# Alternating a group by seven products with a plain group in the feed-forward layers, and moving two splits ahead of top-k

## The chip, the cores and the metric

The kernel runs on one NeuronCore of a Trainium2 chip. The metric is the device time of one execution in microseconds, the median of several runs. A profiled execution gives the trace that is read here.

## The reference, cut to what matters

One input of 256 tokens by 1024 features goes through three layers in float32. Each layer is a mixer with a residual and then the same feed-forward form:

```python
def swiglu(h, w1, w3, w2):
    return (jax.nn.silu(h @ w1) * (h @ w3)) @ w2     # 1024 -> 2816 -> 1024
```

The first mixer is a sparse attention: four index heads score every pair of tokens, `top_k` keeps 64 keys of each query, and eight heads with two key/value groups attend to those keys. Beside it runs a pooling branch. The second mixer is a stick-breaking attention, the third joins a retention and a block-sparse attention. Only the first mixer and the three feed-forward layers are touched.

## The kernel before, in words

**Products in three passes.** Every float32 operand is held as a rounded high part and a low remainder, and `mm3` (L297) issues three matmuls: high by high, high by low, low by high, with the activations (128 by 128) as the loaded operand and 512 weight columns moving. Tokens come in two halves `h` of 128.

**The stream of weights.** `Stream` (L117 on) is a list of loads, sums and pieces written out ahead of time by the `plan_` functions. A load (L185) brings 1 MiB into one of four `w_raw` buffers through SyncE's queue. A piece is 128 by 1024 words: `_split` (L232) makes `w_hi` on ScalarE (L238) and `w_lo` on VectorE (L239), into five buffers each. `advance` (L244) issues loads, sums and splits up to four pieces ahead of the piece that TensorE takes; `tick` (L400) calls it and steps the background tasks (evacuations, transposes) that have come due. A framework then orders each engine's instructions by their place in the program, or by a raised priority, as its own timing finds them ready; each engine runs its list in that order.

**The feed-forward layer.** `ffn` (L602) walks `FF_GROUPS` (L517): hidden columns 0, 512 and 1536 are plain groups, 1024 and 2048 are groups by seven products, 2560 is a plain group of 256 columns. A plain group runs `proj` (L419) for `w1` and for `w3`: four pieces each, and each piece is used for both token halves, twelve matmuls. `gate` (L624) takes the silu on ScalarE, `up` (L629) multiplies on VectorE. Both projections take two of the four `acc` banks of PSUM.

A group by seven products (`block`, L563) treats the two token halves by the two halves of the 1024 inputs as a 2 by 2 matrix product with seven products in place of eight. Each has two pieces, and each piece is used once, six matmuls. Some products use sums of weight blocks. `add_block` (L168) plans three plain loads, the sums `s1` and `s3` and the growths `s2` and `s4`. A sum (L215) is a 1 MiB load by SyncE (L227) and a second one issued by GpSimd that accumulates onto it (L229). A growth is a VectorE addition in place (L222). Two sum buffers exist; `s1`, `s2` and `s4` are one buffer in turn, `s3` is the other. The order of products is 1, 5, 6, 2, 3, 7, 4; `s2` feeds product 6, `s4` feeds product 4. Sums of token blocks (`token_sums`, L530, fourteen VectorE and four ScalarE operations) are made once a layer, after group 0. `snap` and `result` (L651, L656) combine the banks. `turn` (L610) transposes a finished group through the two `misc` banks, in two steps two ticks apart.

**The sparse layer** (L925). It projects the index part, then keys and values (`kv`, L997), queries (`q`, L1015) and the pooling input. `top` (L983) is a chain of eight rounds of max and match-and-replace per token half on VectorE (L989, L990), then the mask (L996). `heads_T` (L689) transposes keys or queries through a `misc` bank and splits them (`kT`, `qT`; ScalarE and VectorE L318).

Of the kernel before, what the change touches and what calls it, by code (L numbers as in the profile page):

```python
# [23 lines left out]
F32 = mybir.dt.float32  # L24
# [5 lines left out]
P = 128  # L30
# [85 lines left out]
class Stream:  # L116
# [51 lines left out]
    def add_block(self, wl, cl, wr, cr):  # L168

        h = KD // 2  # L170
        b11, b12, b21, b22 = (wl, 0, h, cl, 512), (wr, 0, h, cr, 512), (wl, h, h, cl, 512), (wr, h, h, cr, 512)
        l11, l22, l21 = (self._load_of(*b) for b in (b11, b22, b21))
        s1 = self._sum_of(b12, b11)
        s3 = self._sum_of(b12, b22)
        s2 = self._grow(s1, l22)
        s4 = self._grow(s2, l21)
        for q, src in ((1, l11), (5, s1), (6, s2), (2, l21), (3, l22), (7, s3), (4, s4)):
            for k in range(0, h, 2):
                self._piece(src, k * 512, 2, 512, (wl, q, k, cl))
# [89 lines left out]
class Kernel:  # L269
# [149 lines left out]
    def proj(self, n, w, c0, cols, evac, fresh=False, feed=None):  # L419
# [4 lines left out]
        accs = [self.ps_acc(), self.ps_acc()]  # L424
# [9 lines left out]
        while k < KD:  # L434
# [13 lines left out]
            k += kc  # L448
        for i, piece in enumerate(held):
            mms(1, *piece)  # L450
            if i < len(held) - 1:
                self.tick()
        self.run(evac(1, accs[1]))
        self.tick()

# [61 lines left out]
    FF_GROUPS = ((0, 512, False), (512, 512, False), (1024, 512, True), (1536, 512, False), (2048, 512, True), (2560, 256, False))  # L517

    def plan_ffn(self, w1, w3, w2):
        for c0, m, block in self.FF_GROUPS:  # L520
            if block:
                self.st.add_block(w1, c0, w3, c0)
            elif m == 512:
                self.plan_proj(w1, c0, m)
                self.plan_proj(w3, c0, m)
            else:
                self.plan_proj(w1, c0, 2 * m, beside=(w3, c0, m))
# [35 lines left out]
    def block(self, n, sums, wl, c0, wr, snap, result):  # L563
# [21 lines left out]
        after(snap, "x1", x)  # L585
        z = self.ps_acc()
        product(z, 5, True)
        after(snap, "z", z)
        product(x, 6, False)
        after(snap, "x2", x)  # L590
# [3 lines left out]
        product(z, 3, False)  # L594
        after(result, 1, 0, z)
        product(x, 7, False)
        after(snap, "x3", x)
        v = self.ps_acc()
        product(v, 4, True)
        after(result, 0, 1, v)  # L600

    def ffn(self, n, w1, w3, w2, evac):  # L602
        nc = self.nc
        with self.tc.tile_pool(name="ffn", bufs=1) as fp, self.tc.tile_pool(name="ffn2", bufs=2) as f2, \
# [16 lines left out]
            def plain(c0, m):  # L621
                sg, hid = [], []
# [16 lines left out]
                if m == 512:  # L639
                    self.proj(n, w1, c0, m, gate, fresh=c0 == 0)  # L640
                    self.proj(n, w3, c0, m, up)
                else:
                    self.proj(n, w1, c0, 2 * m, both)
                return hid

            def by_block(c0):
                sg = [f2.tile([P, 512], F32, name=f"sg{h}") for h in range(2)]
                hid = [f2.tile([P, 512], F32, name=f"hid{h}") for h in range(2)]
                home = {"x1": sg[0], "x2": hid[0], "x3": sg[1], "z": hid[1]}

                def snap(what, acc):  # L651
                    nc.scalar.copy(home[what], acc)
                    if what == "x3":
                        nc.vector.tensor_sub(hid[1], hid[1], sg[1])

                def result(side, h, acc):  # L656
                    if side == 0:
                        nc.vector.tensor_add(sg[h], acc, sg[h])
                        nc.scalar.activation(sg[h], sg[h], AF.Silu, scale=n["rstd"][:, h:h + 1])
                    else:  # L660
                        nc.vector.tensor_sub(hid[h], acc, hid[h])
                    if side == 1 or h == 1:
                        nc.vector.scalar_tensor_tensor(hid[h], hid[h], n["rstd"][:, h:h + 1], sg[h], op0=OP.mult, op1=OP.mult)

                self.block(n, sums, w1, c0, w3, snap, result)
                return hid

            made = False
# [755 lines left out]
```

## Time and profile before

| what | value |
|---|---|
| median of 3 runs | 1014.12 us (1014.04 to 1014.58) |
| the profiled execution, its own time | 1014.49 us |
| its span, first to last instruction | 1012.7 us |
| mean granted TensorE clock | 0.998 |
| busy: TensorE, VectorE, ScalarE, GpSimd | 995.3, 732.6, 597.5, 86.9 us |
| DMA moved | 193.35 MB, mean 191 GB/s |

A matmul's length in the trace overlaps the next one's; the step from start to start (0.227 to 0.233 us for 128 by 512) is what one costs.

### The profile page before, as it was taken

What the parts mean: (1) busy time and instruction counts of PE and PEld (TensorE: products, weight loads), DVE (VectorE), ACT (ScalarE), POOL (GpSimd) and SP (SyncE); (2) the same over time, 40 slices, a digit from 0 to 9 for tenths busy, and PEclk for the clock granted to TensorE, in tenths of its full rate; (3) what the DMA queues carried; (4) which work ended last, traced back from release to release, by engine and by line L of the source; (5) the groups of instructions that cost most, each with busy time, mean ns of one, the idle gap of its engine ahead of it and who ended that gap; (6) DMA issues with size and microseconds to landing.
All of it is one profiled execution on the core that took longest, in us unless ns stands there. A gap on an engine that the chain in (4) does not pass through costs nothing.

```text
span 1012.7 us, 12657 instructions
## 1 busy us (share of the span) xinstructions
PE 995.3 (98%) x4727; PEld 812.8 (80%) x4727; DVE 732.6 (72%) x1009; ACT 597.5 (59%) x896; POOL 86.9 (9%) x180
## 2 busy tenths in 40 slices
PE   8899999999999999999999999999999999999998
PEld 7677887788788888787878888888887888787886
DVE  6987789884467887789794467666777668879643
ACT  7566666653467876757574366675444465667431
POOL 2500101000030000200000024000020011010000
PEclk9999999999999999999999999999999999999999
DMA  8633959764564324955955536445434559395631
GB/s 298 234 123 104 301 182 281 235 230 168 166 208 167 125 86 136 290 196 178 279 192 193 197 131 208 151 166 202 173 124 173 186 207 307 133 294 198 246 127 42
DMA packets 90286, 193.35 MB, mean 191 GB/s; under 512 B 3440, under 2 KB 16368, under 8 KB 90224
## 3 DMA queue, kind: packets, MB, share of 16 engines
q1 hardware_dynamic: 83456, 179.36, 50.7%
q0 software_dynamic: 6336, 12.58, 6.9%
q8 instruction: 37, 0.61, 0.2%
q10 hardware_dynamic: 432, 0.59, 0.2%
q14 instruction: 25, 0.20, 0.1%
HBM read 191.48 MB, written 1.05 MB: 190 GB/s over the span
## 4 chain that ended last, share of the span: by engine, by line
PE 82%; ACT 8%; DVE 6%; issue 3%; POOL 1%; ACTq 0%; DVEq 0%
PE acc L475 27%; PE acc L303 15%; PE acc L302 15%; PE acc L301 15%; ACT w_hi L238 5%; PE misc L327 3%; DVE w_lo L239 1%; DVE w_sum L222 1%; ACT hT_hi L314 1%; PE misc L301 1%; PE misc L302 1%; PE z L301 1%; PE z L303 1%; PE misc L303 1%; PE z L302 1%
## 5 line engine op out<-in xcount | busy, mean ns | idle before, releaser
L239 DVE TENSOR_TENSOR w_lo<-w_raw,w_hi 128x1024 fp32r<-128x1024 f32 (+1 forms) x313 | 375.8, 1214 | 163.9 <-ACT w_hi L238 162.8
L238 ACT CAST w_hi<-w_raw 128x1024 fp32r<-128x1024 f32 (+1 forms) x313 | 323.5, 1045 | 244.8 <-PE acc L475 109.2
L301 PE MATMUL acc<-w_hi,xT_hi 128*128 128x512 f32 (+2 forms) x776 | 302.3, 392 | 1.1 <-ACT w_hi L238 1.1
L302 PE MATMUL acc<-w_lo,xT_hi 128*128 128x512 f32 (+2 forms) x776 | 301.5, 389 | 0.7 <-DVE w_lo L239 0.5
L303 PE MATMUL acc<-w_hi,xT_lo 128*128 128x512 f32 (+2 forms) x776 | 300.9, 388 | 0.0
L301 PEld LDWEIGHTS acc<-w_hi,xT_hi 128*128 128x128 f32 x776 | 146.2, 188 | 29.7 <-ACT w_hi L238 1.6
L303 PEld LDWEIGHTS acc<-w_hi,xT_lo 128*128 128x128 f32 x776 | 146.1, 188 | 29.3
L302 PEld LDWEIGHTS acc<-w_lo,xT_hi 128*128 128x128 f32 x776 | 146.2, 188 | 28.3 <-DVE w_lo L239 1.3
L475 PE MATMUL acc<-w_hi,hT_hi 128*128 128x512 f32 x264 | 105.1, 398 | 0.0
L475 PE MATMUL acc<-w_lo,hT_hi 128*128 128x512 f32 x264 | 104.1, 394 | 0.0
L475 PE MATMUL acc<-w_hi,hT_lo 128*128 128x512 f32 x264 | 86.9, 395 | 0.0
L238 ACT CAST w_hi<-w_sum 128x1024 fp32r<-128x1024 f32 x48 | 50.0, 1057 | 50.8 <-DVE w_sum L222 25.4
L239 DVE TENSOR_TENSOR w_lo<-w_sum,w_hi 128x1024 fp32r<-128x1024 f32 x48 | 58.1, 1221 | 21.6 <-ACT w_hi L238 21.1
L475 PEld LDWEIGHTS acc<-w_hi,hT_hi 128*128 128x128 f32 x264 | 49.6, 188 | 12.5
L475 PEld LDWEIGHTS acc<-w_hi,hT_lo 128*128 128x128 f32 x264 | 49.6, 188 | 11.7
L475 PEld LDWEIGHTS acc<-w_lo,hT_hi 128*128 128x128 f32 x264 | 49.6, 188 | 10.9
L318 DVE SCALAR_TENSOR_TENSOR xT_lo<-misc,gains,xT_hi 128x128 fp32r<-128x128 f32 (+1 forms) x84 | 27.9, 353 | 24.8 <-ACT xT_hi L317 24.7
L301 PE MATMUL acc<-w_hi,xs 128*128 128x512 f32 x96 | 40.1, 418 | 5.0 <-ACT w_hi L238 5.0
L303 PE MATMUL acc<-w_hi,xs 128*128 128x512 f32 x96 | 37.9, 395 | 0.0
L302 PE MATMUL acc<-w_lo,xs 128*128 128x512 f32 x96 | 37.8, 394 | 0.0
L317 ACT ACTIVATE xT_hi<-misc,gains 128x128 fp32r<-128x128 f32 (+1 forms) x84 | 29.0, 370 | 13.8 <-DVE xT_lo L318 9.0
L371 POOL TENSOR_TENSOR norm_s<-norm_ss 128x1 f32<-128x1 f32 x10 | 4.8, 479 | 343.9 <-ACT junk L367 343.8
(297 smaller groups left out, 1250.1 us busy)
## 6 DMA issues: line engine op xcount, KB each, us to landing
w_raw<-in_ffn_w_dram SPq DMA_DIRECT2D x58, 1024.0 KB, 5.1
w_raw<-in_w_in_dram SPq DMA_DIRECT2D x26, 1024.0 KB, 4.9
w_raw<-in_w_ffn_down_dram SPq DMA_DIRECT2D x11, 1024.0 KB, 5.0
w_raw<-in_w_ffn_gate_dram SPq DMA_DIRECT2D x10, 1024.0 KB, 5.5
w_sum<-in_ffn_w_dram SPq DMA_DIRECT2D x8, 1024.0 KB, 6.4
w_sum<-in_ffn_w_dram POOLq DMA_DIRECT2D x8, 1024.0 KB, 14.6
w_raw<-in_od_w_qkv_dram SPq DMA_DIRECT2D x8, 1024.0 KB, 5.1
w_raw<-in_w_ffn_up_dram SPq DMA_DIRECT2D x8, 1024.0 KB, 5.7
```

Of the source, the lines that this page charges most:

```text
L222: nc.vector.tensor_add(t, t, s["y"]["tile"])
L238: self.pin(nc.scalar.copy(hi, raw))
L239: self.pin(nc.vector.tensor_sub(lo, raw, hi.bitcast(F32)))
L301: self.pin(nc.tensor.matmul(out, ah, bh, start=start, stop=False, skip_group_check=True))
L302: self.pin(nc.tensor.matmul(out, ah, bl, start=False, stop=False, skip_group_check=True))
L303: self.pin(nc.tensor.matmul(out, al, bh, start=False, stop=stop, skip_group_check=True))
L314: nc.scalar.copy(hi, src)
L317: self.pin(nc.scalar.mul(hi, src, scale))
L318: self.pin(nc.vector.scalar_tensor_tensor(lo, src, scale, hi.bitcast(F32), op0=OP.mult, op1=OP.subtract))
L327: self.pin(self.nc.tensor.transpose(out, in_, self.ident))
L371: self.nc.gpsimd.tensor_tensor(s, n["ss"][:, h, 0:1], n["ss"][:, h, 1:2], op=OP.add)
L475: mm = lambda a, b, start, stop: self.nc.tensor.matmul(o, a, b, start=start, stop=stop, skip_group_check=True)
```

## The change

The work and the number of matmuls stay. The four 512-column groups after group 0 become two pairs: plain 512 with seven products 1024, and plain 1536 with seven products 2048. A pair's plan (`add_pair`) alternates one plain piece with one product (two pieces): plain, 1, plain, 5, plain, 3, plain, 2, plain, 6, plain, 7, plain, 4, plain. `proj` and `block` become generators that `ffn` steps in turn. The plain group of a pair accumulates in the two `z` banks (`ps_z`), the seven products in the four `acc` banks. The order of products is 1, 5, 3, 2, 6, 7, 4. The token sums start between the two projections of group 0. In the sparse layer `heads_T` raises the priority of the splits of keys and of queries.

```diff
--- before.py
+++ after.py
@@ -12,7 +12,7 @@


 import heapq
-from contextlib import ExitStack
+from contextlib import ExitStack, nullcontext

 import numpy as np

@@ -165,18 +165,26 @@
         for k in range(0, kc, step):
             self._piece(src, k * n, min(step, kc - k), n, (w, k0 + k, c0))

-    def add_block(self, wl, cl, wr, cr):
+    def add_pair(self, w1, w3, cp, cb):
+

         h = KD // 2
-        b11, b12, b21, b22 = (wl, 0, h, cl, 512), (wr, 0, h, cr, 512), (wl, h, h, cl, 512), (wr, h, h, cr, 512)
-        l11, l22, l21 = (self._load_of(*b) for b in (b11, b22, b21))
+        load = lambda w, k0, c: self._load_of(w, k0, h, c, 512)
+        a0, l11, l22, a1 = load(w1, 0, cp), load(w1, 0, cb), load(w3, h, cb), load(w1, h, cp)
+        l21, b0, b1 = load(w1, h, cb), load(w3, 0, cp), load(w3, h, cp)
+        b11, b12, b22 = (w1, 0, h, cb, 512), (w3, 0, h, cb, 512), (w3, h, h, cb, 512)
         s1 = self._sum_of(b12, b11)
         s3 = self._sum_of(b12, b22)
         s2 = self._grow(s1, l22)
         s4 = self._grow(s2, l21)
-        for q, src in ((1, l11), (5, s1), (6, s2), (2, l21), (3, l22), (7, s3), (4, s4)):
-            for k in range(0, h, 2):
-                self._piece(src, k * 512, 2, 512, (wl, q, k, cl))
+        factors = ((1, l11), (5, s1), (3, l22), (2, l21), (6, s2), (7, s3), (4, s4))
+        plain = [(src, w, k0 + k, k) for src, w, k0 in ((a0, w1, 0), (a1, w1, h), (b0, w3, 0), (b1, w3, h)) for k in (0, 2)]
+        for i, (src, w, k0, k) in enumerate(plain):
+            self._piece(src, k * 512, 2, 512, (w, k0, cp))
+            if i < len(factors):
+                q, src = factors[i]
+                for k in range(0, h, 2):
+                    self._piece(src, k * 512, 2, 512, (w1, q, k, cb))

     @staticmethod
     def _part(w, k0, kc, c0, n):
@@ -416,12 +424,16 @@
         for k0 in range(0, KD, kc):
             self.st.add(w, k0, min(kc, KD - k0), c0, n, beside)

-    def proj(self, n, w, c0, cols, evac, fresh=False, feed=None):
-
-
-
-
-        accs = [self.ps_acc(), self.ps_acc()]
+    def proj(self, *args, **kw):
+        for _ in self.proj_steps(*args, **kw):
+            pass
+
+    def proj_steps(self, n, w, c0, cols, evac, fresh=False, feed=None, bank=None):
+
+
+
+
+        accs = [(bank or self.ps_acc)() for _ in range(2)]

         def mms(h, k, kc, wh, wl):
             for kk in range(k, k + kc):
@@ -446,12 +458,15 @@
                 if k + kc < KD:
                     self.tick()
             k += kc
+            if k < KD:
+                yield
         for i, piece in enumerate(held):
             mms(1, *piece)
             if i < len(held) - 1:
                 self.tick()
         self.run(evac(1, accs[1]))
         self.tick()
+        yield

     def plan_out(self, w, ks):
         for k0 in range(ks[0], ks[-1] + 1, 2):
@@ -514,17 +529,17 @@

-    FF_GROUPS = ((0, 512, False), (512, 512, False), (1024, 512, True), (1536, 512, False), (2048, 512, True), (2560, 256, False))
+    FF_GROUPS = ((0,), (512, 1024), (1536, 2048), (2560,))

     def plan_ffn(self, w1, w3, w2):
-        for c0, m, block in self.FF_GROUPS:
+        for c0, *block in self.FF_GROUPS:
             if block:
-                self.st.add_block(w1, c0, w3, c0)
-            elif m == 512:
-                self.plan_proj(w1, c0, m)
-                self.plan_proj(w3, c0, m)
+                self.st.add_pair(w1, w3, c0, block[0])
+            elif FF - c0 >= 512:
+                self.plan_proj(w1, c0, 512)
+                self.plan_proj(w3, c0, 512)
             else:
-                self.plan_proj(w1, c0, 2 * m, beside=(w3, c0, m))
+                self.plan_proj(w1, c0, 2 * (FF - c0), beside=(w3, c0, FF - c0))
         self.plan_out(w2, list(range(KF)))

     def token_sums(self, n, pool, tmp, out):
@@ -560,7 +575,7 @@
         difference(d, (0, 0), (1, 0))
         done(7, d)

-    def block(self, n, sums, wl, c0, wr, snap, result):
+    def block(self, n, sums, wl, c0, snap, result):

@@ -583,21 +598,29 @@
         x = self.ps_acc()
         product(x, 1, True)
         after(snap, "x1", x)
+        yield
         z = self.ps_acc()
         product(z, 5, True)
         after(snap, "z", z)
-        product(x, 6, False)
-        after(snap, "x2", x)
+        yield
+        product(z, 3, False)
+        self.tick()
+        yield
         w = self.ps_acc()
         product(w, 2, True)
         after(result, 0, 0, w)
-        product(z, 3, False)
+        yield
+        product(x, 6, False)
+        self.run(snap("x2", x))
         after(result, 1, 0, z)
+        yield
         product(x, 7, False)
         after(snap, "x3", x)
+        yield
         v = self.ps_acc()
         product(v, 4, True)
         after(result, 0, 1, v)
+        yield

     def ffn(self, n, w1, w3, w2, evac):
         nc = self.nc
@@ -618,8 +641,8 @@
                     k = c0 // P + j
                     self.evac_split(hh[:, k:k + 2, :], hl[:, k:k + 2, :], tp.rearrange("p (k t) -> p k t", t=T))

-            def plain(c0, m):
-                sg, hid = [], []
+            def plain(c0, m, hid, **kw):
+                sg = []

                 def gate(h, acc):
                     s = f2.tile([P, 512], F32, name=f"sg{h}")
@@ -637,41 +660,57 @@
                     up(h, acc[:, m:])

                 if m == 512:
-                    self.proj(n, w1, c0, m, gate, fresh=c0 == 0)
-                    self.proj(n, w3, c0, m, up)
+                    yield from self.proj_steps(n, w1, c0, m, gate, fresh=c0 == 0, **kw)
+                    if c0 == 0:
+                        made.append(self.spawn(self.token_sums(
+                            n, f2, lambda i: f2.tile([P, 512], F32, name=("sg0", "sg1", "hid0")[i]), sums)))
+                    yield from self.proj_steps(n, w3, c0, m, up, **kw)
                 else:
-                    self.proj(n, w1, c0, 2 * m, both)
-                return hid
-
-            def by_block(c0):
-                sg = [f2.tile([P, 512], F32, name=f"sg{h}") for h in range(2)]
-                hid = [f2.tile([P, 512], F32, name=f"hid{h}") for h in range(2)]
-                home = {"x1": sg[0], "x2": hid[0], "x3": sg[1], "z": hid[1]}
+                    yield from self.proj_steps(n, w1, c0, 2 * m, both, **kw)
+
+            def by_block(c0, hid):
+                tiles = {}
+
+                def home(what):
+                    if what not in tiles:
+                        tiles[what] = f2.tile([P, 512], F32, name=what)
+                        if what[:3] == "hid":
+                            hid[int(what[3])] = tiles[what]
+                    return tiles[what]
+
+                where = {"x1": "sg0", "x2": "hid0", "x3": "sg1", "z": "hid1"}

                 def snap(what, acc):
-                    nc.scalar.copy(home[what], acc)
+                    nc.scalar.copy(home(where[what]), acc)
                     if what == "x3":
-                        nc.vector.tensor_sub(hid[1], hid[1], sg[1])
+                        nc.vector.tensor_sub(hid[1], hid[1], home("sg1"))

                 def result(side, h, acc):
+                    sg = home(f"sg{h}")
                     if side == 0:
-                        nc.vector.tensor_add(sg[h], acc, sg[h])
-                        nc.scalar.activation(sg[h], sg[h], AF.Silu, scale=n["rstd"][:, h:h + 1])
+                        nc.vector.tensor_add(sg, acc, sg)
+                        nc.scalar.activation(sg, sg, AF.Silu, scale=n["rstd"][:, h:h + 1])
                     else:
                         nc.vector.tensor_sub(hid[h], acc, hid[h])
                     if side == 1 or h == 1:
-                        nc.vector.scalar_tensor_tensor(hid[h], hid[h], n["rstd"][:, h:h + 1], sg[h], op0=OP.mult, op1=OP.mult)
-
-                self.block(n, sums, w1, c0, w3, snap, result)
-                return hid
-
-            made = False
-            for c0, m, block in self.FF_GROUPS:
+                        nc.vector.scalar_tensor_tensor(hid[h], hid[h], n["rstd"][:, h:h + 1], sg, op0=OP.mult, op1=OP.mult)
+
+                yield from self.block(n, sums, w1, c0, snap, result)
+
+            made = []
+            for c0, *block in self.FF_GROUPS:
+                m = min(512, FF - c0)
+                hid = []
                 if block:
-                    self.finish([made])
-                hid = by_block(c0) if block else plain(c0, m)
-                if not made:
-                    made = self.spawn(self.token_sums(n, f2, lambda i: f2.tile([P, 512], F32, name=("sg0", "sg1", "hid0")[i]), sums))
+                    self.finish(made)
+                    hid2 = [None, None]
+                    other = by_block(block[0], hid2)
+                    for _ in plain(c0, m, hid, bank=self.ps_z):
+                        next(other, None)
+                    self.spawn(turn(block[0], m, hid2))
+                else:
+                    for _ in plain(c0, m, hid):
+                        pass
                 last = self.spawn(turn(c0, m, hid))
             self.outproj([(w2, k, (hh[:, k], hl[:, k])) for k in range(KF)], evac, need=[last])
         self.st.sum_p = None
@@ -686,13 +725,14 @@
         nc.vector.reduce_sum(ss, sq.rearrange("p (h d) -> p h d", d=64), axis=AX.X)
         self.inv_sqrt(out, ss, 64, EPS, nh)

-    def heads_T(self, flat, nt, gain, outs, h):
+    def heads_T(self, flat, nt, gain, outs, h, first=False):

         tp = self.ps_misc()
         for j in range(nt):
             self.transpose(tp[:, j * P:(j + 1) * P], flat[:, j * P:(j + 1) * P])
         sl = slice(h * P, (h + 1) * P)
-        self.evac_split(outs[0][:, :, sl], outs[1][:, :, sl], tp[:, :nt * P].rearrange("p (j t) -> p j t", t=P), gain)
+        with self.tc.high_priority() if first else nullcontext():
+            self.evac_split(outs[0][:, :, sl], outs[1][:, :, sl], tp[:, :nt * P].rearrange("p (j t) -> p j t", t=P), gain)

     def pair_values(self, oT, v, p0, p1):

@@ -1010,7 +1050,7 @@
                 yield DL["kv_T"]
                 for i in range(2):
                     nc.gpsimd.tensor_copy(vp[i][:, h, :, 64:], vp[i][:, h, :, :64])
-                self.heads_T(kn.rearrange("p h r d -> p (h r d)"), 2, self.gains[:, G_EK:G_EK + 1], kT, h)
+                self.heads_T(kn.rearrange("p h r d -> p (h r d)"), 2, self.gains[:, G_EK:G_EK + 1], kT, h, first=True)

             def q(h, acc):
                 with tc.high_priority():
@@ -1018,7 +1058,7 @@
                     nc.scalar.mul(t, acc, rstd(h))
                     self.head_factors(rq[h], t, 8)
                 yield DL["q_T"]
-                self.heads_T(t, 4, gq8[:, 0:1], qT, h)
+                self.heads_T(t, 4, gq8[:, 0:1], qT, h, first=True)

             def uu(h, acc):
                 nc.scalar.mul(u[:, h], acc, rstd(h))
```

## Rows read from the trace of the kernel before

**Rows 1.** The page, part 1: busy time of TensorE.

```profile
PE 995.3 (98%) x4727; PEld 812.8 (80%) x4727; DVE 732.6 (72%) x1009; ACT 597.5 (59%) x896; POOL 86.9 (9%) x180
```

**Rows 2.** Waits of TensorE over the span, those that the change is near.

```profile
PE acc L301 <- ACT w_hi L238: 6.1, 8, 0.9
PE misc L327 <- DVE kT L318: 3.0, 1, 3.0
```

**Rows 3.** Timeline of TensorE inside the first two groups by seven products.

```profile
151.79 0.40 PE L301 MATMUL acc<-w_hi,xs 128*128 128x512 f32 x1
153.05 0.50 PE L301 MATMUL acc<-w_hi,xs 128*128 128x512 f32 x1 [0.85 <-ACT w_hi L238]
...
197.12 0.50 PE L301 MATMUL acc<-w_hi,xs 128*128 128x512 f32 x1 [0.83 <-ACT w_hi L238]
```

**Rows 4.** Timeline of VectorE and ScalarE in the first of those groups.

```profile
141.44 2.28 DVE L222 TENSOR_TENSOR w_sum<-w_sum,w_raw 128x2048 f32<-128x2048 f32 x1
...
143.84 1.05 ACT L238 CAST w_hi<-w_sum 128x1024 fp32r<-128x1024 f32 x1 [4.23 <-DVE w_sum L222]
...
151.92 3.48 DVE L239 TENSOR_TENSOR w_lo<-w_raw,w_hi 128x1024 fp32r<-128x1024 f32 x3
161.06 0.74 DVE L663 SCALAR_TENSOR_TENSOR hid<-hid,norm_rstd,sg 128x512 f32<-128x512 f32 x1
```

**Rows 5.** Busy time by stretch: PE, PEld, DVE, ACT, POOL, clock, DMA share, GB/s.

```profile
137.00:162.00 25.00, 24.15 (x110) 19.45 (x109) 22.88 (x22) 17.78 (x22) 0.00 (x0) 1.00 0.43 153
```

**Rows 6.** Timeline of TensorE in the sparse layer, around its longest stall.

```profile
41.03 0.39 PE L302 MATMUL acc<-w_lo,xT_hi 128*128 128x512 f32 x1
44.47 0.63 PE L327 MATMUL misc<-ident,q 128*128 128x128 f32 x4 [3.05 <-DVE kT L318]
...
45.40 0.54 PE L302 MATMUL acc<-w_lo,xT_hi 128*128 128x512 f32 x1
...
49.04 0.39 PE L303 MATMUL acc<-w_hi,xT_lo 128*128 128x512 f32 x1
...
50.66 0.39 PE L301 MATMUL acc<-w_hi,xT_hi 128*128 128x512 f32 x1
...
59.34 0.50 PE L727 MATMUL z<-mask,cst_r 128*128 128x512 f32 x1
```

**Rows 7.** Busy time by stretch around that stall; the granted clock before the DMA share.

```profile
41.30:44.40 3.10, 0.12 (x1) 0.00 (x0) 3.10 (x14) 1.07 (x2) 2.61 (x7) 1.00 0.00 0
...
47.00:48.30 1.30, 1.30 (x5) 1.01 (x4) 1.30 (x3) 1.04 (x2) 1.22 (x2) 0.50 0.37 91
```

**Rows 8.** Timeline of ScalarE and VectorE there: keys, weight parts, queries, mask.

```profile
34.67 0.47 ACT L317 ACTIVATE kT<-misc,gains 128x256 fp32r<-128x256 f32 x1
...
43.84 0.47 DVE L318 SCALAR_TENSOR_TENSOR kT<-misc,gains,kT 128x256 fp32r<-128x256 f32 x1
...
45.35 1.21 DVE L239 TENSOR_TENSOR w_lo<-w_raw,w_hi 128x1024 fp32r<-128x1024 f32 x1
...
48.34 0.74 DVE L318 SCALAR_TENSOR_TENSOR qT<-misc,gq,qT 128x512 fp32r<-128x512 f32 x1
...
52.85 0.42 DVE L996 TENSOR_TENSOR mask<-sc,cst_r 128x256 fp32r<-128x256 f32 x1
```

**Rows 9.** Line 229, GpSimd's accumulating loads: all twelve, then those at 164 and 166 us.

```profile
DMA to landing us min/median/max: 9.2/14.6/19.5
...
DMA to landing us min/median/max: 14.0/14.0/14.0
...
DMA to landing us min/median/max: 19.3/19.3/19.3
```

**Rows 10.** Line 227's plain loads, and where the second group's sums are issued.

```profile
DMA to landing us min/median/max: 5.1/6.4/10.0
...
158.30 3.24 SPq L227 DMA_DIRECT2D w_sum<-in_ffn_w_dram  x2
...
164.23 1.28 POOL L229 DMA_DIRECT2D w_sum<-in_ffn_w_dram  x1 [53.52 <-DMA w_sum<-in_ffn_w_dram]
```

## Prediction

> **What bounds the kernel now.** I read the page first: TensorE is busy 98% of the span [rows 1], and the change keeps every matmul. So the change is worth what TensorE idles near it, less what it makes TensorE idle anew. The table of waits gives two spells near the change: a chain of waits for `w_hi` and one wait of 3.0 us for `kT` [rows 2]. The timeline places six of the eight `w_hi` waits, 0.83 to 0.85 us each, one in each group by seven products (three layers, two groups); the other two lie in the first 9 us (the first two of the six: [rows 3]).
>
> Why they are there is seen on the other engines. Inside a group by seven products a piece feeds only six matmuls, 6 x 0.232 = 1.4 us, while its remainder costs VectorE 1.13 us (the step in three that took 3.48 us), and the growth of a sum 2.2 us more. ScalarE stood 4.23 us because product 6 follows product 5 and its weights must first be grown [rows 4]. VectorE is busy 22.9 of 25 us in such a stretch [rows 5], so the four pieces of lead are used up and TensorE runs dry.
>
> In the sparse layer TensorE stops after 41.03 us: the queries' transposes need a `misc` bank that holds keys not yet split [rows 6]. When it starts again the granted clock is 0.50, the lower of its levels [rows 7]. The keys' first split was ready on ScalarE at 35.1 us, and VectorE took its half at 43.84 us, behind the two chains of top-k [rows 8].
>
> For the new order I looked last at the sums' loads: how long the accumulating ones take, first and second of two [rows 9], and when their buffers came free [rows 10].
>
> **Part 1, the pairs.** Removed: the six stalls. From 151.79 to 153.05 is 1.26 us where 0.23 is due, so 1.03 each [rows 3], **6 x 1.03 = -6.2 us**. They should go because product 6 now comes eight pieces after product 5 and product 4 three after its growth, and because VectorE's work is spread. A pair needs 22 remainders (22 x 1.13 = 24.9), two growths (4.4), and about 12 evacuations at 0.60 to 0.66 (7.5), 36.8 us, beside 180 matmuls x 0.23 = 41.4 us. ScalarE's load is less.
>
> Added, each a new wait:
>
> - *The `z` banks.* The next pair's first projection writes the bank that the last `up` reads. TensorE gives it the other half's six matmuls, 1.4 us; `up` takes 0.74 and may stand behind one remainder of 1.13 [rows 4]. Bounds 0 and 0.8 us per layer, once each. The short end is nearer, since the pair's last piece has no product beside it: 0.3 x 3 = **+0.9**. Within a pair the second projection reaches the bank after a product, 4 us later: nothing, unless ScalarE is stopped.
> - *The token sums* now run in 11 us of the second projection of group 0, no longer in 22 us of a plain group. Fourteen operations of at most 0.74 us, 10.4 us, stand in front of remainders there. The cover is four plain pieces, 11 us, already split when that projection starts. Bounds 0 and 1.5 us per layer (two operations too late); I take 0.2 x 3 = **+0.6**.
> - *The second pair's first sum.* Before, a plain group of 22 us lay between two groups by seven. Now a pair follows a pair. The sum buffer that it reuses is free after the second piece of product 7 is split. With the full lead this is when TensorE starts piece 13 of 22, plus one split (2.4 us) and one growth (2.2 us). TensorE needs the sum nine pieces after product 7. From piece 13 to there are 108 matmuls, 24.8 us; less about 3 to 4.5 us, some 21 us remain. Needed: 5.9 us from the plain load's issue to GpSimd's (158.30 to 164.23; plain loads take 5.1 to 10.0), then 14.0 us for the first of two accumulating loads [rows 9, 10], and 1.2 us for `w_hi`: 21.1 us. That just fits, so here nothing is lost directly. But ScalarE reaches this `w_hi` early and stands in it, and behind it in its queue stand the evacuations of both groups' transposes, two groups at once in two `misc` banks. The second step of transposes then waits on TensorE. Bounds: 0, and 25.0 + 1.2 - 21 = 5.2 us per layer if the load behaves like the second of two (161.2, when the later of two issues began, plus 25.0 is its landing at 186.2). It is nearest to the first of two, so I take 0.8 x 3 = **+2.4**.
>
> The raw loads keep their number; the latest buffer release, that of the plain group's last load, leaves it seven pieces (13 us) before use against 5 us. SyncE's queue issues the same 1 MiB transfers in a new order, GpSimd has nothing else in these stretches, and the rounding of operands is untouched: no cost.
>
> A rule bears on that sum. The two accumulating loads at 164 and 166 us landed after 14.0 and 19.3 us [rows 9]. The Trainium skill (DMA: Bandwidth & Descriptors, Queues, rings and completion order) says that each DMA engine takes turns between the queues that have work, a packet at a time. By that rule a lone accumulating load, its fellow issued some 5 us later, would share only with SyncE's loads and come nearer to 9.2 us; the term of 2.4 us would be zero and the time 1005.7.
>
> **Part 2, keys and queries.** Removed: 41.03 to 44.47 is 3.44 us where 0.23 is due, 3.2 us. Then the slow clock: from 45.40 to 49.04 seven matmuls and four transposes take 3.64 us, where 7 x 0.228 + 0.38 = 1.98 is due, 1.7 us [rows 6, 7]. Together **-4.9 us**. What is late next: the last piece of the layer's pooling projection, which TensorE began at 50.66 and would reach at 45.8, second matmul at 46.0. Its `w_lo` ended at 45.35 + 1.21 = 46.56 [rows 8]. The keys' splits stood ahead of it before too, but now the queries' two, 0.66 each, may pass in front. So it comes at 46.6 to 47.9, and 0.5 to 1.9 us are lost; with one of the two in front, **+1.2**. The moved operations push top-k by at most 2 us; the mask of the second half ended at 53.3 and is needed at about 54.4 (59.34 less 4.9 [rows 6]), so that hides, by a little. If the engine order kept the keys behind top-k, 0 would be gained: that is the lower bound.
>
> **Sum.** -6.2 + 0.9 + 0.6 + 2.4 - 4.9 + 1.2 = -6.0 us from the profiled execution's 1014.49, or 1008.5. Its span is 1012.7, so 1.8 us lie around it and stay. The median is 0.4 lower: **1008.1 us**. A measurement of this kernel tells about 0.2% (2 us) from no change.
>
> **Rivals.**
>
> - *All new waits are covered*: -6.2 - 4.4 (the `w_lo` wait at its low end) gives 1003.5. For it: VectorE has 4.6 us to spare in a pair. The Trainium skill's rule above would bring about the largest part of this case. Against it: the sum's load fits by less than its own spread. Chance 0.18.
> - *The first stalls are given back*: transposes or sum cost 2 us per layer and boundary, 6 us in all, and only part 2 remains, 1014.1 - 6.2 + 6.0 + 1.5 - 3.7 = 1011.7. For it: two groups now turn at once through two banks. Chance 0.17.
> - *Slower: the second pair's first sum.* One mechanism: its accumulating load takes as long as the second of two, 5.2 us lost in each layer, 15.6 against -9.9 from the rest with its small costs at 0.9 + 0.6: 1014.1 - 9.9 + 1.5 + 15.6 = 1021.3. It decides from 2.8 us per layer on, when the sum lands 22.6 us or more after its buffer is free. For it: twelve loads spread from 9.2 to 19.5 us. Against it: its fellow is issued after it. Chance 0.10.
> - *The change does not do what it says*: the framework's order leaves keys behind top-k, and VectorE, no faster in total, runs dry elsewhere. About 1013.5. For it: every engine's order is the framework's, not the program's. Against it: raised priorities already moved the head factors into top-k. Chance 0.07.
>
> **How the numbers follow.** My forecast has 0.48, with its own range 1005.5 to 1010.5. The range that holds 8 in 10 leaves out the slower rival, the no-effect rival and a little of each end: 1003.0 to 1013.0. Faster by over 0.2% (below 1012.1): forecast, the first rival and most of the second, 0.79. Within 0.2%: the rest of the second, the no-effect rival and small cases of the slower one, 0.12. Slower: 0.09.
>
> **What would show it.** In the profile after: no wait of 0.8 us for `w_hi` inside the pairs; no wait for `kT` at 41 us, full clock there, and a short wait for `w_lo` instead. Each new cost has its sign: TensorE waiting for `hid` or for VectorE's `up` at a pair's first matmuls; for `hT_lo` at transposes early in the second pair; ScalarE idle for a transfer into `w_sum` there. The prediction is wrong if that last wait is over 3 us, or if six waits for weights are still there.

## The result and the profile after

The changed kernel takes 1039.86 us (median of 4 runs, 1036.70 to 1040.03) against 1014.35 us of the kernel before on the same chip: a ratio of 1.0244, 95% interval 1.0224 to 1.0264, slower by 25.5 us. The forecast was 1008.1 us, its range 1003.0 to 1013.0. The profiled execution took 1036.70 us with a span of 1034.9 us, 22.2 us more than the span before.

Page of the changed kernel, part 1, and the shares of its chain, the work that ended last, followed back from the last instruction (it answers to [rows 1]):

```profile
PE 1003.2 (97%) x4727; PEld 818.4 (79%) x4727; DVE 732.6 (71%) x1009; ACT 602.0 (58%) x896; POOL 85.4 (8%) x180
...
PE 74%; DVE 9%; DMA 8%; ACT 4%; issue 3%; POOL 2%; ACTq 0%; DVEq 0%; POOLq 0%
```

The matmuls are the same 4727. TensorE is busy 7.9 us longer over them, ScalarE 4.5 us, VectorE and GpSimd no longer. DMA has 8% of the chain, where it had none before. The waits of the changed kernel (total us, times, longest), the rows that answer to [rows 2]:

```profile
ACT w_hi L246 <- DMA w_sum<-in_ffn_w_dram: 20.3, 3, 9.1
PE misc L335 <- DVE hT_lo L323: 16.4, 6, 5.3
ACT w_hi L246 <- DMA w_sum<-in_w_ffn_gate_dram: 11.8, 2, 9.1
PE z L309 <- ACT at_m L779: 3.6, 1, 3.6
PE misc L335 <- DVE hid L654: 1.8, 2, 1.3
```

The six waits for `w_hi` inside the groups by seven products are gone, and so is the wait for `kT`. In their place TensorE waits 16.4 us for `hT_lo` at transposes, twice in each layer, and 3.6 us for a `z` bank in the sparse layer. ScalarE waits for transfers into `w_sum`: 7.8, 9.1 and 9.1 us at the second pair's first sum of the three layers, and 3.44 and 2.65 us at the first pair's first sum of the first and third layer.

**The transposes.** First the transfer, in the timelines of SyncE's queue and of GpSimd. The buffer was freed at 149.87, when VectorE ended the last split that read it:

```profile
149.90 5.03 SPq L235 DMA_DIRECT2D w_sum<-in_ffn_w_dram  x2
```
```profile
157.66 1.28 POOL L237 DMA_DIRECT2D w_sum<-in_ffn_w_dram  x1 [45.98 <-DVE w_lo L247]
160.38 1.27 POOL L237 DMA_DIRECT2D w_sum<-in_ffn_w_dram  x1 [1.45 <-DMA w_sum<-in_ffn_w_dram]
```

GpSimd's first load landed after 12.4 us, at 170.06, and ScalarE started on the sum at 170.18. ScalarE, VectorE and TensorE around that moment (timeline: start, us, instruction, idle before and what ended it):

```profile
161.64 0.72 ACT L692 ACTIVATE sg<-sg,norm_rstd 128x512 f32<-128x512 f32 x1 [0.53 <-DVE sg L691]
170.18 1.04 ACT L246 CAST w_hi<-w_sum 128x1024 fp32r<-128x1024 f32 x1 [7.82 <-DMA w_sum<-in_ffn_w_dram]
171.13 0.58 ACT L322 CAST hT_hi<-misc 128x512 fp32r<-128x512 f32 x1
...
171.26 1.23 DVE L247 TENSOR_TENSOR w_lo<-w_sum,w_hi 128x1024 fp32r<-128x1024 f32 x1 [6.54 <-ACT w_hi L246]
172.40 0.68 DVE L323 TENSOR_TENSOR hT_lo<-misc,hT_hi 128x512 fp32r<-128x512 f32 x1
...
168.75 0.39 PE L311 MATMUL acc<-w_hi,xT_lo 128*128 128x512 f32 x1
173.14 1.11 PE L335 MATMUL misc<-ident,hid 128*128 128x128 f32 x4 [4.00 <-DVE hT_lo L323]
174.88 1.11 PE L335 MATMUL misc<-ident,hid 128*128 128x128 f32 x4 [0.62 <-DVE hT_lo L323]
175.64 0.77 PE L309 MATMUL z<-w_hi,xT_hi 128*128 128x512 f32 x1
...
178.35 0.45 PE L309 MATMUL z<-w_hi,xT_hi 128*128 128x512 f32 x1
```

ScalarE stood 7.82 us in the sum's `w_hi`. The evacuation of the first transposes (`hT_hi`) stood behind it, on VectorE `hT_lo` stood behind the sum's `w_lo`, both `misc` banks stayed full, and TensorE stopped after 168.75, at the transposes; the matmuls behind them in its queue, from 175.64, needed none of this. When it starts again the granted clock is low (windows: length, busy and count of each engine, PEclk, DMA share, GB/s):

```profile
173.10:176.00 2.90, 2.24 (x9) 1.84 (x10) 2.90 (x3) 1.96 (x4) 0.00 (x0) 0.50 1.09 261
176.00:179.00 3.00, 3.00 (x9) 2.33 (x9) 3.00 (x4) 1.53 (x2) 0.00 (x0) 0.59 0.78 258
```

In this layer that is 4.16 us (168.75 to 173.14 less 0.23), 1.39 and 0.41 us at the two steps of transposes (0.35 due for each four), and 1.32 us for six matmuls from 175.64 to 178.35 (2.71 against 6 x 0.232): 7.3 us. In the other two layers the first stop is 5.4 and 5.5 us, and the same steps come to 8.6 and 9.2 us, so the three layers make about 25 us.

**The sparse layer.** TensorE no longer stops at 41 us, but later (timelines of TensorE, VectorE and ScalarE):

```profile
53.93 0.38 PE L1074 MATMUL misc<-pool_c,u 128*128 128x128 f32 x2
57.88 0.38 PE L309 MATMUL z<-kT,qT 64*128 64x256 f32 x1 [3.57 <-ACT at_m L779]
...
52.55 1.24 DVE L247 TENSOR_TENSOR w_lo<-w_raw,w_hi 128x1024 fp32r<-128x1024 f32 x1
54.02 0.43 DVE L1036 TENSOR_TENSOR mask<-sc,cst_r 128x256 fp32r<-128x256 f32 x1
54.37 1.28 DVE L771 TENSOR_REDUCE at_mx<-z 128x4 f32<-128x512 f32 x2
55.76 0.17 DVE L774 SCALAR_TENSOR_TENSOR at_nb<-at_mx,rq 128x8 f32<-128x8 f32 x1
...
55.96 0.46 ACT L779 ACTIVATE at_m<-z,at_nb,rq 128x128 f32<-128x128 f32 x1 [3.72 <-DVE at_nb L774]
```

The second half's logits need the `z` banks. ScalarE's exponentials of the first half hold them, and these wait for the maxima (`at_mx`, `at_nb`). The maxima stand on VectorE behind the rest of top-k and four `w_lo` splits of the output projection, of which the last is shown. In the kernel before, the maxima came no sooner, but TensorE reached these logits later:

```profile
55.71 0.17 DVE L734 SCALAR_TENSOR_TENSOR at_nb<-at_mx,rq 128x8 f32<-128x8 f32 x1
...
58.44 0.38 PE L301 MATMUL z<-kT,qT 64*128 64x256 f32 x1
```

So TensorE got here about 4 us earlier than before, while `at_nb` stayed where it was.

### The profile page after: what moved, and what is told of

It reads as the page before. It is cut to its first block, busy times and chain, and to the rows that moved or that the text cites. A ratio compares the mean times of both kernels' runs of the same rounds, so it can differ in the third digit from the quotient of the medians.

```text
span 1034.9 us, 12659 instructions
## 1 busy us (share of the span) xinstructions
PE 1003.2 (97%) x4727; PEld 818.4 (79%) x4727; DVE 732.6 (71%) x1009; ACT 602.0 (58%) x896; POOL 85.4 (8%) x180
## 3 DMA queue, kind: packets, MB, share of 16 engines
HBM read 191.48 MB, written 1.05 MB: 186 GB/s over the span
## 4 chain that ended last, share of the span: by engine, by line
PE 74%; DVE 9%; DMA 8%; ACT 4%; issue 3%; POOL 2%; ACTq 0%; DVEq 0%; POOLq 0%
PE acc L490 26%; PE acc L309 10%; PE acc L311 10%; PE acc L310 10%; DMA w_sum<-in_ffn_w_dram 5%; DVE w_lo L247 4%; PE z L311 3%; PE z L309 3%; PE z L310 3%; PE misc L335 3%; DMA w_sum<-in_w_ffn_gate_dram 2%; ACT w_hi L246 2%; DMA w_sum<-in_w_ffn_up_dram 1%; DVE w_sum L230 1%; PE misc L309 1%
## 5 line engine op out<-in xcount | busy, mean ns | idle before, releaser
L309 PE MATMUL acc<-w_hi,xT_hi 128*128 128x512 f32 (+2 forms) x584 | 229.5, 393 | 1.0 <-ACT w_hi L246 1.0
L310 PE MATMUL acc<-w_lo,xT_hi 128*128 128x512 f32 (+2 forms) x584 | 225.9, 387 | 1.1 <-DVE w_lo L247 0.9
L311 PE MATMUL acc<-w_hi,xT_lo 128*128 128x512 f32 (+2 forms) x584 | 225.4, 386 | 0.0
L309 PEld LDWEIGHTS acc<-w_hi,xT_hi 128*128 128x128 f32 x584 | 109.8, 188 | 22.2 <-ACT w_hi L246 1.6
L311 PEld LDWEIGHTS acc<-w_hi,xT_lo 128*128 128x128 f32 x584 | 109.7, 188 | 21.9
L309 PE MATMUL z<-w_hi,xT_hi 128*128 128x512 f32 x192 | 77.5, 405 | 0.0
L311 PE MATMUL z<-w_hi,xT_lo 128*128 128x512 f32 x192 | 76.9, 400 | 0.0
L310 PE MATMUL z<-w_lo,xT_hi 128*128 128x512 f32 x192 | 76.6, 399 | 0.0
L309 PEld LDWEIGHTS z<-w_hi,xT_hi 128*128 128x128 f32 x192 | 37.5, 195 | 8.1
L310 PEld LDWEIGHTS z<-w_lo,xT_hi 128*128 128x128 f32 x192 | 37.3, 194 | 8.2 <-DVE w_lo L247 0.3
```

The source lines that it names most:

```text
L309: self.pin(nc.tensor.matmul(out, ah, bh, start=start, stop=False, skip_group_check=True))
L310: self.pin(nc.tensor.matmul(out, ah, bl, start=False, stop=False, skip_group_check=True))
L311: self.pin(nc.tensor.matmul(out, al, bh, start=False, stop=stop, skip_group_check=True))
```

## The experiments

The theory was that the second pair's first sum comes too late for ScalarE's queue, and that the transposes, not the sum's own product, pay for it. The rivals: two groups that turn at once through two `misc` banks cost it by themselves; or part 2 costs it.

| kernel | median us | ratio to before, 95% interval |
|---|---|---|
| pairs alone | 1036.76 | 1.0218 (1.0185 to 1.0250) |
| part 2 alone | 1017.00 | 1.0023 (1.0013 to 1.0033) |
| change, third sum buffer | 1014.93 | 0.9999 (0.9990 to 1.0008) |
| change, accumulation left out | 1014.91 | 0.9999 (0.9988 to 1.0011) |
| change, transposes apart | 1027.76 | 1.0133 (1.0119 to 1.0147) |
| change, fellow left out (two runs) | 1037.55 | 1.0217 (1.0187 to 1.0247) |
| part 2, splits behind the maxima | 1011.42 | 0.9961 (0.9948 to 0.9975) |
| pairs, third buffer | 1013.63 | 0.9974 (0.9964 to 0.9985) |
| the same, group 0's transposes later | 1009.11 | 0.9941 (0.9929 to 0.9954) |
| the change with all three repairs | 1005.50 | 0.9904 (0.9890 to 0.9917) |

### The two parts alone

Each run was measured beside the kernel before, whose median was between 1014.56 and 1015.09 us.

The pairs without part 2:

```diff
-self.heads_T(kn..., kT, h, first=True)
+self.heads_T(kn..., kT, h)
-self.heads_T(t, 4, gq8[:, 0:1], qT, h, first=True)
+self.heads_T(t, 4, gq8[:, 0:1], qT, h)
```

> The pairs alone, the sparse layer as before. Theory (the late first sum of the second pair costs the time, part 2 is worth about nothing): within 2 us of the changed kernel, 1037 to 1041 us, with the transposes waiting for hT_lo 4 to 5.5 us in each feed-forward layer. Rival that part 2 brings the loss: back near the kernel before, 1006 to 1014 us. If part 2 were worth the 3.7 us of the prediction: 1043 to 1044 us.

1036.76 us, 0.2 us below the theory's range: the pairs alone lose 22.2 us, nearly all of the loss. Its four executions lie between 1032.48 and 1041.34 us, so that figure is known to a few us only. The waits for `hT_lo` are there (4.95 to 6.72 us, the first of each layer). Part 2 alone, the same two lines added to the kernel before:

> Part 2 alone on the kernel before. Theory (the stall for kT turns into a stall of TensorE at the second half's logits, which wait for a z bank that ScalarE's exponentials of the first half hold, because at_mx stands behind the splits for the output projection on VectorE): 1014 to 1016 us, a wait of 3 to 4 us near 54 us. Prediction's own term (a gain of 3.7 us): 1010 to 1011 us. Rival that part 2 costs the time: above 1030 us.

1017.00 us, above the theory's figure and 6 us above the prediction's: part 2 by itself costs 2.4 us. Its stop is the one seen above; the row of its waits, and TensorE's window behind the stop (length, busy and count, PEclk, DMA share, GB/s):

```profile
PE z L301 <- ACT at_m L740: 3.6, 1, 3.6
```
```profile
60.00:65.00 5.00, 5.00 (x17) 0.50 0.00 0
```

### The sum in time

```diff
-SUMS = 2
+SUMS = 3
```

The loads of sums were also put on a list apart from the growths; that edit moves no instruction, the third buffer alone gives every engine the same list.

> The changed kernel with a third sum buffer, the loads of sums no longer queued behind growths. Theory (the sum's late load stops ScalarE, and the evacuations behind it): ScalarE's wait of 8 to 9 us for w_sum goes, and with it the transposes' wait for hT_lo of 4 to 5.3 us and the slow clock behind it in all three layers; 1009 to 1015 us. Rival that two groups turning at once in two misc banks is enough by itself: the waits for hT_lo stay over 3 us per layer, 1030 to 1040 us.

1014.93 us, at the theory's upper end: 24.9 us come back, as much as the rows above gave for the stops. GpSimd's load for this sum is now issued at 134.52, not 157.66. The timelines of ScalarE and TensorE with three buffers, at the same place:

```profile
166.40 1.05 ACT L250 CAST w_hi<-w_sum 128x1024 fp32r<-128x1024 f32 x1 [0.46 <-PE z L318]
168.29 0.59 ACT L329 CAST hT_hi<-misc 128x512 fp32r<-128x512 f32 x1 [0.84 <-PE misc L342]
...
167.55 0.71 PE L342 MATMUL misc<-ident,hid 128*128 128x128 f32 x5
169.93 0.49 PE L342 MATMUL misc<-ident,hid 128*128 128x128 f32 x3
172.56 1.24 PE L342 MATMUL misc<-ident,hid 128*128 128x128 f32 x8
```

Both groups still turn at once through two banks, and no transpose waits for `hT_lo` in any of the layers. So the rival of the banks falls as a sufficient cause. The third buffer could act in another way than through time, so the load itself was taken away:

```diff
-            for spec in s["specs"][1:]:
+            for spec in s["specs"][1:] if self.taken % 4 != 3 else ():
```

> The changed kernel, two sum buffers, with GpSimd's accumulating load of the second pair's first sum left out (so that sum holds one block only: a part of the computation is left out). Theory (what is late is that load's landing, 12.4 us after its issue): the sum is there at about 157.5 us instead of 170, ScalarE's wait for w_sum and the transposes' wait for hT_lo go, 1012 to 1016 us like the third buffer. Rival (two groups turning at once): unchanged, above 1030 us.

1014.91 us, the same as with a third buffer, and again no transpose waits for `hT_lo`. What is late is the landing of the accumulating load.

### The transposes apart

```diff
-                    self.spawn(turn(block[0], m, hid2))
+                    self.spawn(turn(block[0], m, hid2), 6)
```

> The changed kernel with the transposes of the group by seven products started six ticks after those of its plain partner; the sums as they are. Theory (late sum): the transposes no longer wait, but ScalarE still stands 8 to 9 us for w_sum, and TensorE then runs into the late w_hi of that sum or of pieces behind it: 1 to 4 us per layer, 1012 to 1028 us. Rival (bank shortage alone): the loss is gone whole, 1008 to 1012 us, with no wait of TensorE for w_hi there.

1027.76 us, at the theory's upper end. ScalarE still stands 8.64 us. Now TensorE works on until it needs what the sum holds up (timeline):

```profile
172.73 0.39 PE L311 MATMUL z<-w_hi,xT_lo 128*128 128x512 f32 x1
173.29 0.50 PE L309 MATMUL acc<-w_hi,xs 128*128 128x512 f32 x1 [0.17 <-ACT w_hi L246]
174.55 0.50 PE L310 MATMUL acc<-w_lo,xs 128*128 128x512 f32 x1 [0.76 <-DVE w_lo L247]
...
177.56 0.48 PE L309 MATMUL z<-w_hi,xT_hi 128*128 128x512 f32 x1
180.22 0.50 PE L310 MATMUL z<-w_lo,xT_hi 128*128 128x512 f32 x1 [2.18 <-DVE w_lo L247]
```

The `w_hi` came almost in time (0.17 us). Then 1.03 us go for the sum's `w_lo` and 2.43 us for the next plain piece's `w_lo`, which stands behind a growth on VectorE. That is 3.5 us a layer, 10.4 of the 12.8 us by which this kernel is above the one with three buffers. The same two stops come in the other layers, and there the granted clock falls behind the second (0.56 from 496 to 499 us, 0.70 from 915 to 918 us), which costs 1.6 us more in each. In the first layer, after the same stop of 2.18 us, it stayed at 1.00. That makes 13.6 us in all. So about half of the 24.9 us is lateness of the sum itself, and half what the transposes make of it.

### Does the fellow stretch the load?

```diff
-            for spec in s["specs"][1:]:
+            for spec in s["specs"][1:] if self.taken % 4 != 0 else ():
```

> The changed kernel with the accumulating load of the second pair's second sum left out (that sum holds one block only), so that the first sum's accumulating load runs without its fellow beside it. If the fellow's packets are what stretches it (the queues take turns): it lands after about 9.2 us instead of 12.4, 3 us earlier in each layer, 1026 to 1032 us. If SyncE's loads or the accumulation itself set its time: it lands after 12 us or more, 1035 to 1040 us.

1037.55 us, the second answer. The load's own row, issued at 159.14 (least, median and greatest are of this one load):

```profile
DMA to landing us min/median/max: 12.3/12.3/12.3
```

With its fellow, in the changed kernel, the load issued at 157.66 took 12.4 us. So the fellow does not stretch it. The fellow itself, issued at 160.38, took 17.7 us: while the first ran, GpSimd's queue moved 1.21 MB, of which 1.05 MB were the first. This load of 12.3 us had 2.57 MB of SyncE's loads beside it; one of 9.2 us in the kernel with three buffers, issued at 161.84, had 1.33 MB. No run changed that traffic alone, so what sets the length of these loads is not shown.

### Repairing the sparse layer

The splits for the output projection are issued with a lead of one piece during the pooling projection, and their `w_lo` is held behind `at_nb`:

```diff
+            self.st.asp = 1
             self.proj(n, wi, 1092, 512, uu)
...
             self.finish(po)
+            self.st.asp = AHEAD
...
+            if first and h == 0:
+                self.st.tc, self.st.after = self.tc, i
...
-        self.pin(nc.vector.tensor_sub(lo, raw, hi.bitcast(F32)))
+        with self.tc.issue_after(self.after.ins) if self.after else nullcontext():
+            self.pin(nc.vector.tensor_sub(lo, raw, hi.bitcast(F32)))
```

> Part 2 alone on the kernel before, and the output projection's four w_lo splits held behind the first half's maxima (at_nb) on VectorE. Theory (those four splits, 4 x 1.13 us, are what kept the maxima, and so the z banks, until 56 us): at_nb comes 4 to 5 us earlier, the stop of 3.6 us before the second half's logits goes, and with it the slow clock after it; 1010.5 to 1013.5 us. Rival (VectorE's whole queue of this stretch is the bound, the order inside it does not matter): the stop moves to the copies for the pooling branch or to w_lo of the output projection, 1015 to 1017.5 us.

1011.42 us, beside 1015.09 of the kernel before. On VectorE `at_nb` now comes at 52.18 (56.06 with part 2 alone), and TensorE has no stop and full clock from 50 to 60 us (timeline of VectorE, windows of TensorE):

```profile
50.78 1.28 DVE L734 TENSOR_REDUCE at_mx<-z 128x4 f32<-128x512 f32 x2
52.18 0.17 DVE L737 SCALAR_TENSOR_TENSOR at_nb<-at_mx,rq 128x8 f32<-128x8 f32 x1
52.26 2.35 DVE L241 TENSOR_TENSOR w_lo<-w_raw,w_hi 128x1024 fp32r<-128x1024 f32 x2
```
```profile
50.00:55.00 5.00, 5.00 (x27) 1.00 0.42 174
55.00:60.00 5.00, 5.00 (x28) 1.00 0.64 210
```

VectorE does the same 1009 operations as with part 2 alone, and is as long busy over them (732.3 and 732.5 us). The order inside its queue was the cause; the rival, VectorE's whole load, falls.

### Repairing the pairs, and everything together

The pairs with three sum buffers and the sparse layer as before:

> The pairs with the third sum buffer, the sparse layer as before. Theory (six stalls gone, 6.1 us; about 2.5 us given back where group 0's transposes wait for hid behind the token sums): 1010.5 to 1013 us. Rival that the pairs themselves are worth nothing even with their sums in time: 1014 to 1015 us.

1013.63 us, just above the range and below the rival's. Four of its seven executions lie at 1013.6 to 1013.7 us, three at 1011.4 to 1011.9, and the profiled one is of the three. TensorE still waits twice for `hid`, 0.44 us in the first layer and 1.38 us in the third. The same with group 0's transposes three ticks later:

```diff
-                last = self.spawn(turn(c0, m, hid))
+                last = self.spawn(turn(c0, m, hid), 3 if c0 == 0 else 0)
```

> As the pairs with the third sum buffer and the old sparse layer, and group 0's transposes three ticks later. Theory (the wait for hid is one of place, not of VectorE's whole load): the waits of 1.1 us for hid in the first and third feed-forward layer go and nothing takes their place, 1008.5 to 1011 us. Rival (VectorE is behind by the ten us of token sums and stays behind): the same time as without the delay, with a wait for w_lo or w_hi in place of that for hid.

1009.11 us. The waits are 0.3 us in all, and nothing takes their place:

```profile
PE misc L342 <- DVE hid L661: 0.3, 1, 0.3
```

The medians differ by 4.5 us, the two profiled executions (1011.53 and 1009.51 us) by 2.0, so the size of this repair is known only to within that. The whole change with the three repairs:

> The whole change with three repairs: third sum buffer, group 0's transposes three ticks later, the output projection's splits behind the first half's maxima. Theory (the three costs are separate and add): 1004.5 to 1009 us. Rival (one of the repairs does not hold or they meet on VectorE): 1010 to 1014 us.

1005.50 us, 1% below the kernel before. The costs were separate, as the theory had it: the repaired pairs gained 6.0 us and the repaired part 2 gained 3.7, and together they gain 9.6. Part 1 of the page, and TensorE's longest waits for weight parts, of which none lies in the pairs (these are in the first 10 us and at 47 us):

```profile
PE 993.3 (99%) x4727; PEld 813.0 (81%) x4727; DVE 731.5 (73%) x1009; ACT 602.7 (60%) x896; POOL 85.6 (9%) x180
```
```profile
PE acc L318 <- ACT w_hi L251: 0.9, 2, 0.8
PE acc L319 <- DVE w_lo L253: 0.9, 2, 0.5
```

## Why the prediction was wrong, and where it was right

**The six stalls** (-6.2 us): right. They are gone. The kernel with all repairs lies 5.9 us below the one with part 2 repaired alone (1005.50 and 1011.42), and the repaired pairs without part 2 lie 6.0 us below the kernel before.

**The `z` banks in the pairs** (+0.9): too dear; no wait on them was seen there.

**The token sums** (+0.6): too small, and in the wrong place. No remainder came late; `up` stood behind the sums on VectorE, and group 0's transposes waited for its `hid`, 1.8 us in all.

**The second pair's first sum** (+2.4): this step failed, and it decided the result. The transfer as a whole was forecast well, 19.9 us from the free buffer to the landing (5.9 + 14.0), 20.2 measured, but with luck: GpSimd issued 7.8 us after the buffer was free, and the load then took 12.4, so two errors of opposite sign cancelled. The time until TensorE reaches the sum's own product was forecast well too: 21 us, and 21.9 with the transposes apart (151.08, the issue, to 172.96). What failed is "some 21 us remain ... That just fits, so here nothing is lost directly". That is the deadline of the wrong consumer. The first step that needs anything behind the sum's `w_hi` is the second transposes of the pair before, due at 168.98. From the landing to the free bank it takes the sum's `w_hi`, `hT_hi`, the sum's `w_lo` and `hT_lo`, 170.18 to 173.08, 2.9 us. So the sum had to land 168.98 - 149.90 - 2.9 = 16.2 us after its buffer was free. It came 4.0 us later than that, which is the 4.00 us that TensorE waited. The prediction named these transposes, but priced them at 0.8 us a layer by nearness to a bound and bounded them by the sum's own lateness, 5.2 us. Measured are 8.3 us a layer (24.9 / 3), beyond the bound, since a stop of 4 to 5.5 us also brought the low clock and a second stop behind the first. The same low clock was in the rows before, after the stop for `kT` [rows 7], and was counted there, but not here. The prediction's own sign of being wrong, ScalarE idle for a transfer into `w_sum` for over 3 us, came with 7.8 to 9.1 us in each layer.

**The rule on turns.** The Trainium skill (DMA: Bandwidth & Descriptors, Queues, rings and completion order) has each DMA engine take turns between queues. The prediction drew from this that a load without its fellow would come nearer to 9.2 us. Left alone it took 12.3 us. Both loads are in GpSimd's queue, and the rule speaks of turns between queues: the reading was wrong, and the run says nothing against the rule.

**Part 2** (-4.9 + 1.2): the removed stall and the `w_lo` wait came as forecast (45.74 to 46.54 where 0.23 is due, 0.57 us, near the low end of 0.5 to 1.9), but the gain was lost at the next late thing. The prediction took that to be the last piece of the pooling projection, and let the mask hide "by a little". The late one was the first half's maxima, behind splits that nobody needed yet; alone, part 2 cost 2.4 us. With the maxima ahead it gains 3.7 us (1015.09 to 1011.42). That this is the prediction's own figure is luck: 4.9 less the measured 0.6 would be 4.3, and TensorE also waits 0.71 us for `pT` at 60.93, which the prediction did not have.

**The rivals.** The slower one, at 0.10, named the right place, the right wait and the right queue. Its mechanism did not come: the load took 12.4 us, less than the first of two before. It took the load for the open quantity, where the deadline was, and so came to 1021.3 us; the sum landed 20.2 us after its buffer was free, under the 22.6 us from which that rival was to decide, and the loss decided all the same. The rival "the first stalls are given back" spoke of two groups through two banks; that is harmless while ScalarE keeps up.

Added up for the profiled execution, -6 for the stalls, +1.8 for `hid`, +25 for the stops at the transposes and +2.4 for part 2 make 23 us; the spans differ by 22.2. With the three costs away the change takes 1005.50 us, 9.6 us less than the kernel before, where the terms of gain less the measured `w_lo` wait make 10.5. So the terms of gain were right to about 1 us, and the forecast failed on what stands in line behind a late instruction.

## What to carry to other kernels

When a transfer may be late, list what stands behind its first user on that in-order engine, and take the earliest due time in that list as the deadline, not that of the product the transfer is for. Price a possible stop of TensorE with the slow clock after it. When a stall is taken out by moving work ahead on a full engine, look at what else that engine holds back in the next ten microseconds, and put work that is due later behind it.

## What the runs showed of the hardware

An accumulating load took about twice the DMA engines' time of a plain one. In the kernel with the fellow left out, from 159 to 172 us, the queues' shares of the 16 engines' time were (queue, packets, MB, share; SyncE's loads are q1, GpSimd's is q0):

```profile
q1 hardware_dynamic: 1419, 2.82, 59.2%
q0 software_dynamic: 528, 1.05, 46.7%
```

Of 13 us, 1.05 MB that accumulate took 6.1 us, and 2.82 MB of plain loads 7.7 us, 2.9 us for each 1.05 MB: a factor of 2.1. (The shares add to more than 100%, so the packets' times overlap.) Over the whole span of the changed kernel, 1034.9 us, the same rows of the page give 5.6 us per MB on GpSimd's queue and 2.9 us on SyncE's, a factor of 1.9:

```profile
q1 hardware_dynamic: 83456, 179.36, 50.0%
q0 software_dynamic: 6336, 12.58, 6.8%
```

The Trainium skill (Collectives: The Full Stack, The bandwidth ceiling: the fold count and why AG ≠ RS ≠ AR) says of a reduce-scatter that its add needs two source reads, which makes it half as fast as an all-gather. The factor here agrees with that; that the reads are the reason is not shown by any run.

The granted clock of the start differs between executions. The kernel with three sum buffers, and the kernel before, in the same stretch (windows):

```profile
8.00:11.00 3.00, 2.35 (x11) 1.86 (x10) 2.39 (x5) 2.17 (x5) 0.00 (x0) 0.78 0.59 187
```
```profile
8.00:11.00 3.00, 2.36 (x15) 1.91 (x14) 2.00 (x3) 2.05 (x6) 0.00 (x0) 1.00 0.59 193
```

The profiled execution of the kernel with three buffers ended its `w_lo` wait in the pooling projection at 48.63 us, the changed kernel's, whose clock was 1.00 in that stretch, at 46.54, with the same instructions before it: about 2 us that no edit made.
